# The last input load moved from SyncE's DMA queue to ScalarE's, behind two waits

## The chip, the cores and the metric

The kernel runs on one core of a Trainium2 chip. The metric is device time in microseconds (us), the median of several executions. The profile shows one execution, taken by the hardware profiler; its span is somewhat shorter than the time of that execution, and the table below gives both.

Engines are named as in the profile: PE is TensorE (matmuls), PEld its weight loads, DVE is VectorE, ACT is ScalarE, POOL is GpSimd, SP is SyncE. SP computes nothing here; it issues DMAs. The 16 DMA engines of the core move the data, whichever engine issued them.

## The reference

```
q, k : (8 batches, 8 heads, 512 rows, 64) float32
out[b, h] = q[b, h] @ k[b, h].T * (1 / sqrt(64))      # (8, 8, 512, 512) float32
```

The inputs are 8.4 MB each, the output is 67.1 MB.

## The kernel before

**Units and groups.** The work is cut into four *units* of two batches (`UNITS = 4`). A unit has one load of k (x = 0) and one of q (x = 1), each 2 MB as 128 partitions of 16 KB. They are called k0, q0 to k3, q3 here. Every unit gives four *groups* of output (`ALL = 16` groups, g = 0 to 15). A group is one store of 4 MB: 128 partitions, two rows of 16 KB each. The stores are called store 0 to store 15.

**Buffers.** There are three big buffers in SBUF of 4 MB each (`bigs`). A buffer holds either the raw q and k of a unit, or the finished output of a group:

```
    def xf(v):
        return bigs[(0, 1, 2, 1)[v]].rearrange("p x i k -> p (x i k)").rearrange(
...
    def store_buffer(g):
        return bigs[(0, 2, 1)[g % 3]]
```

So units 0, 1, 2 are loaded into buffers 0, 1, 2, and unit 3 goes into buffer 1 once unit 1 has been read out of it. Group 0 writes its output into buffer 0, group 1 into buffer 2 (where unit 2 was), group 2 into buffer 1 (where unit 3 was), group 3 into buffer 0 again, and so on.

**Stages.** POOL casts what has been loaded to bf16 (line 122, two casts for each load, `ready` is raised by one when both are done). PE transposes the cast data through PSUM (`turn`, line 130), eight transposes at a time. ACT and DVE copy the transposed words into `kT` and `qz` (`move`, line 184), each for its half of the partitions. PE then makes the scores of a group as eight pairs of matmuls of 128x512 (`scores`, line 145). Even pairs are taken out of PSUM, scaled, by ACT (line 209), odd pairs by DVE (line 212), into the buffer of the group. Each raises its semaphore, `act` or `dve`, by one for every pair.

**Order.** Each engine has an order written out by hand; an engine waits in it until a semaphore has reached a constant.

- SP: six loads k0 to q2 at once; then it waits for `ready >= 3` (both casts of k1 done) and issues k3 over k1; then for `ready >= 4` (casts of q1 done) and issues q3 over q1; then for each group it waits until ACT and DVE have raised their semaphores by four each, and issues the store (lines 95 and 96). At the end it waits for the stores.
- POOL: the casts in the order k0, q0, ..., k3, q3, each behind the landing of its load.
- PE: in each group the first three pairs, then the transposes of the chunk four groups ahead (`c = g + CHUNKS`), then the other five pairs. Before the second matmul of a group it makes sure that the group's buffer is free:

```
                if g < 3:
                    pe.wait_ge(sem["ready"], (2, 6, 8)[g])
                else:
                    pe.wait_ge(store_sems[g % 3], g // 3 * 16)
```

  Group 1 thus waits for the casts of q2 (`ready >= 6`), group 2 for those of q3 (`ready >= 8`), the later ones for the store that used the buffer last (group 3 for store 0, group 4 for store 1).
- ACT and DVE: `evacuator`, with `parity` 0 for ACT and 1 for DVE. It first moves the first four chunks; then, group by group, it evicts its four pairs of the eight, with the moves of one chunk in between.

Of the kernel before, what the change touches and what calls it, by code (L numbers as in the profile page):

```python
# [5 lines left out]
def kernel(  # L6
# [5 lines left out]
    nc = tc.nc  # L12
# [3 lines left out]
    UNITS = B // 2  # L16
# [21 lines left out]
    sem = {name: nc.alloc_semaphore(name) for name in names}  # L38
    load_sems = [nc.alloc_semaphore(f"load{n}") for n in range(2 * UNITS)]
# [3 lines left out]
    q_r = q.rearrange("(v b) g (m j) d -> v (b g m) (j d)", b=2, j=R)  # L43
    k_r = k.rearrange("(v b) g (m j) d -> v (b g m) (j d)", b=2, j=R)
# [25 lines left out]
    def xf(v):  # L70
        return bigs[(0, 1, 2, 1)[v]].rearrange("p x i k -> p (x i k)").rearrange(
            "p (x s c) -> p x s c", x=2, s=2)

    def store_buffer(g):
        return bigs[(0, 2, 1)[g % 3]]

    def load(v, x):
        return nc.sync.dma_start(out=xf(v)[:, x],
                                 in_=(k_r, q_r)[x][v].rearrange("p (s c) -> p s c", s=2)
                                 ).then_inc(load_sems[2 * v + x], 16)  # L80


    tc.no_tile_sem_insts.add(load(0, 0).ins.name)
    tc.close()
    tc.compile()  # L85


    for n in range(1, 2 * (UNITS - 1)):
        load(n // 2, n % 2)
    for x in range(2):  # L90
        nc.sync.wait_ge(sem["ready"], 3 + x)
        load(UNITS - 1, x)
    for g in range(ALL):
        nc.sync.wait_ge(sem["act"], 4 * g + 4)
        nc.sync.wait_ge(sem["dve"], 4 * g + 4)  # L95
# [59 lines left out]
    for g in range(ALL):  # L155
        c = g + CHUNKS
# [12 lines left out]
    def move(copy, c, s, tile_):  # L169
        v, t = divmod(c, CHUNKS)  # L170
        n0 = v % 2 * N
        h0 = t % 2 * W
        if t < 2:
            src = tile_[half(s)].rearrange("d j (n h m) -> d h n m j", n=N, h=2)
        else:
            src = tile_[half(s)].rearrange("d (i jj) (n h m) -> d h i n m jj", jj=JJ, n=N, h=2)
            h0 = t % 2 * IW
        for h in range(2):
            if t < 2:
                dst = kw[half(h), n0:n0 + N, :, s, h0:h0 + W]  # L180
            else:
                dst = qw[half(h), n0:n0 + N, h0:h0 + IW, h * U // 2:(h + 1) * U // 2].rearrange(
                    "d n i (m s jj) -> d s i n m jj", s=2, jj=JJ)[:, s]
            copy(out=dst, in_=src[:, h]).then_inc(sem["moved"], 1)  # L184

    def evacuator(engine, copy, scaled, parity, done, freed):
        if parity:
            for v in range(2):
                engine.memset(qz[:, v * N:(v + 1) * N], 0.0).then_inc(sem["zeroed"], 1)  # L189
        for c in range(CHUNKS):  # L190
            engine.wait_ge(sem["turn"], c + 1)
            if c == 2:
                engine.wait_ge(sem["zeroed"], 2)
            move(copy, c, parity, first[c])
        count = 0
        for g in range(ALL):
            o = store_buffer(g)
            for p in range(parity, PAIRS, 2):
                x, i = p // 4, p % 4 * 2
                count += 1  # L200
                engine.wait_ge(done, count)
                scaled(o[:, x, i:i + 2, :], pss[(PAIRS * g + p) % 3]).then_inc(freed, 1)
                c = g + CHUNKS
                if p in (1, 2) and c < ALL:
                    engine.wait_ge(sem["turn"], c + 1)
                    move(copy, c, parity, tp)

    evacuator(nc.scalar, nc.scalar.copy,
              lambda o, ps: nc.scalar.mul(out=o, in_=ps, mul=scale),  # L209
              0, sem["pe_act"], sem["act"])  # L210
    evacuator(nc.vector, nc.vector.tensor_copy,
              lambda o, ps: nc.vector.tensor_scalar(out=o, in0=ps, scalar1=scale, scalar2=None,  # L212
                                                    op0=mult),
# [31 lines left out]
```

## Time and profile before

| What | Value |
|---|---|
| Time, median of 3 runs | 201.15 us (201.14 to 201.38) |
| The profiled execution's own time | 201.16 us |
| Its span | 199.8 us |
| Granted TensorE clock, mean | 0.827 of full speed |
| Busy: PE, DVE, ACT, POOL | 98.2, 106.1, 84.7, 39.5 us |
| Moved by DMA | 83.95 MB, mean 420 GB/s |
| Read from HBM, written to HBM | 16.78 MB, 67.11 MB |
| Issue to landing, median: store, k load, q load | 21.8, 15.4, 17.8 us |

How to read it: the page gives the busy time of each engine, then a strip in 40 slices of 5 us (a digit is the busy share of a slice in tenths, and a row gives the rate of the DMA engines in GB/s), then the queues, the chain of work that ended last, and groups of instructions by line. Every line of the chain and of a timeline begins with its start in us and its length in us. "Issue to landing" is the time from the start of the issuing instruction until the last part of the data has been reported as landed; with several transfers queued it holds the waiting in the queue too. `q1` is the queue on which SP's DMAs run.

### The profile page before, as it was taken

To read this page: it belongs to the slowest core of one execution; us is meant where nothing else is said; L and a number is where in the kernel's file an instruction comes from. 1 tells how busy PE (TensorE), PEld (TensorE's weight loads), DVE (VectorE), ACT (ScalarE), POOL (GpSimd) and SP (SyncE) were. 2 spreads that over 40 slices of the span, in tenths; PEclk is the share of its full clock that TensorE was granted. 3 is DMA by queue.
4 is the path that set the end of the run, shared out by engine and by line. 5 is a ranking of instruction groups with operands and counts; after the bars stand their busy time and mean duration, and the time that the engine had idled before them with its cause. 6 is when DMAs were issued, how large, how long until landed. Compare 5 with 4: busy or idle time off the path is not lost.

```text
span 199.8 us, 1074 instructions
## 1 busy us (share of the span) xinstructions
PE 98.2 (49%) x377; PEld 46.7 (23%) x384; DVE 106.1 (53%) x98; ACT 84.7 (42%) x97; POOL 39.5 (20%) x22
## 2 busy tenths in 40 slices
PE   0027660375695637676547646873737373720000
PEld 0026530141442314243124313330202020200000
DVE  4815691074798928476917682767364545440000
ACT  2004670264686726465626653664444343520000
POOL 1299999986000000000000000000000000000000
PEclk9999996578799978889957995799696969685555
DMA  6999999999999999999999999999999999999996
GB/s 207 433 436 426 430 433 433 430 387 430 426 443 426 426 425 431 439 430 423 426 443 433 426 423 436 436 430 423 430 443 430 423 426 436 433 426 430 436 426 275
DMA packets 5509, 83.95 MB, mean 420 GB/s; under 512 B 384, under 2 KB 384, under 8 KB 384
## 3 DMA queue, kind: packets, MB, share of 16 engines
q1 hardware_dynamic: 5504, 83.89, 98.7%
q8 instruction: 3, 0.05, 0.1%
q14 instruction: 2, 0.02, 0.0%
HBM read 16.78 MB, written 67.11 MB: 420 GB/s over the span
## 4 chain that ended last, share of the span: by engine, by line
DMA 53%; DVE 12%; POOL 12%; PE 9%; issue 1%; ACT 1%; SPq 0%
DMA out_dram<-big 42%; POOL xb L122 12%; DVE big L212 10%; DMA big<-in_q_dram 8%; PE ps L145 7%; DMA big<-in_k_dram 4%; PE tp L130 3%; DVE qz L184 2%; DVE kT L184 1%; ACT big L209 1%; SPq L95 0%
## 5 line engine op out<-in xcount | busy, mean ns | idle before, releaser
L145 PE MATMUL ps<-kT,qz 128*128 128x512 bf16 x249 | 78.4, 447 | 63.0 <-DMA out_dram<-big 31.1
L212 DVE TENSOR_SCALAR big<-ps 128x1024 f32<-128x1024 f32 x64 | 77.0, 1223 | 52.0 <-PE ps L145 49.9
L209 ACT ACTIVATE big<-ps 128x1024 f32<-128x1024 f32 x64 | 64.9, 1024 | 71.1 <-PE ps L145 67.9
L145 PEld LDWEIGHTS ps<-kT,qz 128*128 128x128 bf16 x256 | 24.8, 108 | 109.7 <-DMA out_dram<-big 34.5
L122 POOL CAST xb<-big 128x2048 bf16<-128x2048 f32 x16 | 38.8, 2466 | 7.0 <-DMA big<-in_k_dram 6.0
L130 PE MATMUL tp<-identity,xb 128*128 128x128 f32 x104 | 18.9, 343 | 13.6 <-POOL xb L122 13.6
L130 PEld LDWEIGHTS tp<-identity,xb 128*128 128x128 f32 x104 | 17.2, 184 | 17.6 <-issue 16.5
L184 DVE COPY kT<-tp 64x512 f32<-64x512 f32 x14 | 9.7, 694 | 9.0 <-PE tp L130 8.5
L184 ACT COPY kT<-tp 64x512 f32<-64x512 f32 x14 | 8.1, 577 | 14.1 <-PE tp L130 14.0
L184 DVE COPY qz<-tp 64x512 f32<-64x512 f32 x12 | 8.3, 694 | 4.4 <-PE tp L130 4.1
L189 DVE MEMSET qz<- 128x4096 uint32 x2 | 6.9, 3472 | 3.6 <-PEq L85 2.8
L184 ACT COPY qz<-tp 64x512 f32<-64x512 f32 x12 | 7.5, 622 | 2.0 <-PE tp L130 1.8
L130 PE MATMUL ps<-identity,xb 128*128 128x128 f32 x24 | 5.4, 412 | 1.2 <-POOL xb L122 1.2
L130 PEld LDWEIGHTS ps<-identity,xb 128*128 128x128 f32 x24 | 5.0, 226 | 1.6 <-POOL xb L122 1.6
L184 DVE COPY qz<-ps 64x512 f32<-64x512 f32 x4 | 2.8, 695 | 1.9 <-PE ps L130 1.7
L184 ACT COPY qz<-ps 64x512 f32<-64x512 f32 x4 | 2.5, 626 | 2.2 <-PE ps L130 2.2
L184 ACT ACT_TABLE_LOAD x1 | 1.3, 1283 | 1.9 <-PEq L85 1.9
L184 DVE COPY kT<-ps 64x512 f32<-64x512 f32 x2 | 1.4, 694 | 0.3 <-PE ps L130 0.3
L184 ACT COPY kT<-ps 64x512 f32<-64x512 f32 x2 | 1.2, 578 | 0.5 <-PE ps L130 0.5
L102 POOL MEMSET identity<- 128x128 f32 x1 | 0.2, 205 | 1.5 <-POOLq L85 1.5
L104 POOL TENSOR_SCALAR_AFFINE_SELECT identity<-identity 128x128 f32<-128x128 f32 x1 | 0.3, 294 | 0.2 <-POOL identity L102 0.2
L229 POOL MEMSET const-float32-0.0<- 128x1 f32 x1 | 0.1, 100 | 0.2 <-issue 0.2
(3 smaller groups left out, 0.3 us busy)
## 6 DMA issues: line engine op xcount, KB each, us to landing
out_dram<-big SPq DMA_DIRECT2D x16, 4096.0 KB, 21.8
big<-in_k_dram SPq DMA_DIRECT2D x4, 2048.0 KB, 15.4
big<-in_q_dram SPq DMA_DIRECT2D x4, 2048.0 KB, 17.8
```

Of the source, the lines that this page charges most:

```text
L102: nc.gpsimd.memset(identity, 0.0).then_inc(sem["ident"], 1)
L104: nc.gpsimd.affine_select(out=identity, in_=identity, compare_op=mybir.AluOpType.not_equal, fill=1.0, base=0, pattern=[[-1, P]], channel_m ...
L122: cast = nc.gpsimd.tensor_copy(out=dst, in_=src)
L130: ins = pe.transpose(out=dst[:, w], identity=identity, in_=xw[:, c % SLOTS * W + w])
L145: ins = pe.matmul(out=pss[pair % 3][:, w, :], lhsT=qz[:, n, i + w], rhs=keys[:, n], start=True, stop=True)
L184: copy(out=dst, in_=src[:, h]).then_inc(sem["moved"], 1)
L189: engine.memset(qz[:, v * N:(v + 1) * N], 0.0).then_inc(sem["zeroed"], 1)
L209: lambda o, ps: nc.scalar.mul(out=o, in_=ps, mul=scale),
L212: lambda o, ps: nc.vector.tensor_scalar(out=o, in0=ps, scalar1=scale, scalar2=None, op0=mult),
L229: nc = _bacc.Bacc("TRN2", target_bir_lowering=False, num_devices=1)
```

## The change

`load` gets the issuing engine as an argument. SP's order loses the wait for `ready >= 4` and the load of q3: it goes from k3 straight to the stores. ACT's order gets three things between its last eviction of group 0 and its first of group 1: the wait for `ready >= 4`, a wait for the landing of k3 (`load_sems[6] >= 16`), and the issue of q3 on ACT's own DMA queue. The data, the buffers and all other waits are as before.

```
-    def load(v, x):
-        return nc.sync.dma_start(out=xf(v)[:, x],
-                                 in_=(k_r, q_r)[x][v].rearrange("p (s c) -> p s c", s=2)
-                                 ).then_inc(load_sems[2 * v + x], 16)
+    def load(v, x, queue=nc.sync):
+        return queue.dma_start(out=xf(v)[:, x],
+                               in_=(k_r, q_r)[x][v].rearrange("p (s c) -> p s c", s=2)
+                               ).then_inc(load_sems[2 * v + x], 16)
...
-    for x in range(2):
-        nc.sync.wait_ge(sem["ready"], 3 + x)
-        load(UNITS - 1, x)
+    nc.sync.wait_ge(sem["ready"], 3)
+    load(UNITS - 1, 0)
     for g in range(ALL):
         nc.sync.wait_ge(sem["act"], 4 * g + 4)
         nc.sync.wait_ge(sem["dve"], 4 * g + 4)
...
             for p in range(parity, PAIRS, 2):
                 x, i = p // 4, p % 4 * 2
+                if g == 1 and p == 0:
+                    engine.wait_ge(sem["ready"], 4)
+                    engine.wait_ge(load_sems[2 * UNITS - 2], 16)
+                    load(UNITS - 1, 1, engine)
                 count += 1
                 engine.wait_ge(done, count)
                 scaled(o[:, x, i:i + 2, :], pss[(PAIRS * g + p) % 3]).then_inc(freed, 1)
```

## The prediction

> **What bounds the kernel now.** I first read the head of the page: the busy strip of the DMA engines, the rate and the queue.
>
> ```profile
> span 199.8 us, 1074 instructions
> ...
> DMA  6999999999999999999999999999999999999996
> GB/s 207 433 436 426 430 433 433 430 387 430 426 443 426 426 425 431 439 430 423 426 443 433 426 423 436 436 430 423 430 443 430 423 426 436 433 426 430 436 426 275
> ...
> q1 hardware_dynamic: 5504, 83.89, 98.7%
> ```
>
> The 16 DMA engines are busy in every slice but the first and the last, at about 430 GB/s, and one queue (SP's) carries everything. 83.89 MB at 430 GB/s is 195 us of the 199.8. So the transfers are the bound: the kernel is lengthened only by an idle stretch of the DMA engines or by a slower rate, and shortened only by removing such a stretch or a dip. There is one dip in the middle (387, slice 9), which the windows view places:
>
> ```profile
> 36.00:40.00 4.00, 2.01 (x5) 0.81 (x6) 0.52 (x1) 1.02 (x1) 3.92 (x2) 0.50 1.03 438
> 40.00:42.00 2.00, 2.00 (x10) 1.79 (x9) 0.71 (x1) 1.02 (x1) 2.00 (x2) 0.50 0.96 319
> 42.00:52.00 10.00, 6.30 (x26) 3.19 (x24) 6.19 (x6) 5.26 (x6) 5.72 (x3) 0.84 1.00 429
> ```
>
> The last column is GB/s. 319 instead of 430 for 2 us is 0.5 us lost, as the last load gives way to the first store.
>
> Next, who needs the moved load (q3: input q, fourth unit). The chain of waits has it, and the timelines of SP and ACT have the issues around it:
>
> ```profile
> 28.23 15.33 DMA big<-in_q_dram
> 43.57 0.05 issue
> 43.62 4.85 POOL xb L122 x2
> 48.47 0.05 issue
> 48.52 1.96 PE ps L145 x5
> ...
> 57.28 0.03 issue
> ```
>
> ```profile
> 23.32 0.33 SPq L78 DMA_DIRECT2D big<-in_k_dram  x1
> 28.23 0.33 SPq L78 DMA_DIRECT2D big<-in_q_dram  x1
> ```
>
> ```profile
> 30.95 0.40 SPq L96 DMA_DIRECT2D out_dram<-big  x1
> ```
>
> ```profile
> 57.32 0.37 SPq L96 DMA_DIRECT2D out_dram<-big  x1
> ```
>
> ```profile
> 29.20 1.03 ACT L209 ACTIVATE big<-ps 128x1024 f32<-128x1024 f32 x1 [1.06 <-PE ps L145]
> 38.63 1.02 ACT L209 ACTIVATE big<-ps 128x1024 f32<-128x1024 f32 x1 [8.40 <-PE ps L145]
> ```
>
> Columns: start, length, what. q3 lands at 43.57; POOL casts it until 48.47; only then may TensorE go past the first matmul of group 2 (ready >= 8, since group 2's results overwrite the buffer that q3 was cast from); 57.32 issues store 2. The chain up to there is serial. It is harmless now because transfers are queued ahead: by the DMA view split by time, k3 lands 14.6 us after 23.32 (37.9), store 0 22.3 us after 30.95 (53.3), store 1 16.4 us after 47.15 (63.6), store 2 16.0 us after 57.32 (73.3), store 3 19.0 us after 63.93. Store 1's data ends about 61.9 (below), so store 2, issued 57.32, comes 4.6 us early. **That slack is what the change spends.**
>
> **What the Trainium skill says.** (1) "DMA: Bandwidth & Descriptors", section "Issuing engines are not separate DMA queues": DMAs of all issuing engines run on the same 16 DMA engines and interleave; a second issuer saves only issue time. The trace before has one queue, so it shows neither; its rate leaves no idle engine to fill. (2) Same page, "Where 436 GB/s comes from": a ceiling of 435 GB/s. The trace agrees: 423 to 443 by slice. (3) Same page, "Queues, rings and completion order": each DMA engine takes turns between the queues that have work, a packet at a time, a packet being typically 9-17 descriptors. No run here shows how long a turn is. A load is 128 rows of 16 KB, 8 per engine, a store 16 per engine, so a turn may be one 16 KB descriptor or a whole transfer's share. This is my main unknown. (4) Same page, "Latency and other measured facts": about 0.6 us to the first byte. The trace differs: the first load is issued at 0.74, and the DMA view cut by time has no packet before 1.75 and one in 1.75:1.80, so I use 1.0 us.
>
> **The change, part by part.**
>
> *SP loses a wait and an issue.* SP no longer waits for ready >= 4 (28.22) and issues q3 (0.33 us). SP's next work, store 0, waits for the evictions of group 0 and goes at 30.95 in either case: worth 0. But store 0 now stands directly behind k3 in SP's queue, and the 16 engines, leaving k3 at about 37.0 (it lands 37.9), go straight to its 9.8 us of data (4.19 MB at 429). No gap arises there, since it was issued 6 us earlier.
>
> *ACT gains two waits and an issue.* ACT is done with group 0 at 29.20 + 1.03 = 30.23; ready >= 4 holds since 28.22, k3's landing comes at 37.95. ACT then issues at about 38.0, for 0.33 to 0.40 us (SP's rows), until 38.4. Behind it in ACT's order is its first eviction of group 1, which starts at 38.63 anyhow, since TensorE itself waits for ready >= 6 until 37.98. Cost 0; at worst, if ACT's issue takes 1 us, 0.8 us late for group 1. Those who wait for that eviction are TensorE (it frees PSUM) and SP (store 1). Store 1 goes at 47.15 and is needed when store 0 and q3 end, after 51, so 4 us cover it.
>
> *q3 shares the engines with store 0.* Issue 38.0 + 1.0 = 39.0 first packets. With turns of one 16 KB descriptor q3 gets half of 430 GB/s: 2.10 MB at 215 GB/s = 9.8 us, so 48.8, and about 1.0 for the spread over engines and the completion (k3: data end near 37.0, landing 37.95): **q3 lands at about 49.8 instead of 43.57, 6.2 us later.** Bounds: it can't beat the whole rate, 39.0 + 4.9 + 1.0 = 44.9; if store 0's share is drained first it starts at 46.8 and lands at 46.8 + 4.9 + 1.0 = 52.7; if mixed reads and writes ran all the time at the dip's 319 GB/s, 39.0 + 4.19 MB/319 + 1.0 = 53.1. I take 49.8, since a packet in the page's count (5504 for 83.89 MB) is one 16 KB row.
>
> *The serial chain moves by the same amount.* Casts 49.85 to 54.7 (2 x 2.42), group 2 from 54.75, then 57.32 - 48.47 = 8.85 us of its own to the issue: 63.6. Its data start at 63.6 + 1.0 = 64.6.
>
> *What the engines have meanwhile.* From 37.0: store 0, q3 and store 1, 10.49 MB at 429 = 24.4 us, to 61.4; before, with the dip's 0.5, to 61.9. So the engines are idle from about 61.4 to 64.6, **some 3 us**. The break-even is q3 landing at 64.6 - 61.9 = 2.7 us before 49.8, 47.1: any later and each us costs a us.
>
> *Nothing gives it back, nothing adds to it.* After store 2 groups follow at about 6.6 us (57.32 to 63.93), transfers at 9.8. Group 3 needs store 0's landing (53), is ready at 70.2, store 2's data last to 74.4; group 4 needs store 1 (63) and is ready by 77, needed at 84. The order before returns, late by the gap. The bubble cannot be made up, for the engines have no other slack.
>
> Sum: transfers after store 1 start at 64.6 instead of 61.9, +2.7 us. The profiled execution took 201.16 us, 1.3 around its span of 199.8; the median is 201.15, so nothing to shift. 201.16 + 2.7 = **203.9 us**. The uncertainty of landing (49.3 to 50.6) gives 203.4 to 204.7.
>
> **The rivals.**
>
> *Turns of a whole share.* q3 waits for store 0 on every engine and lands at 52.7; group 2 and store 2 move 2.9 us further: 206.8. For it speaks the skill's 9-17 descriptors, the count of a load or store per engine with its completion; against it that rows are counted singly.
>
> *Mixed traffic is slow.* The dip's rate throughout the shared stretch: landing 53.1, so 207.2. For it speaks the 319 GB/s; against it that one changeover was over in 2 us.
>
> *The new queue is served ahead (the other side).* If q3 gets well over half of each engine, it lands at 44.9 to 47.1, store 2 is in the queue before store 1's data end, there is no bubble, and the dip's 0.5 us may go as the load no longer ends against the store: 200.6 to 201.2. It decides from a landing before 47.1. Against: nothing prefers a queue.
>
> *The change doesn't do what it says.* If ACT got through its waits later than 38.0, q3 would slip one for one; its instructions ahead end at 30.23, so I see no reason. Nor can the transfers be beside each other for nothing: no rate is free.
>
> **How the numbers follow.** Fair turns 0.66 (203.9), whole share 0.16 (206.8), slow mixing 0.08 (207.2), served ahead 0.10, half of that within 0.2% and half faster. 0.2%, 0.4 us, is about what a measurement of this kernel can tell from no change. The range 202.2 to 207.1 goes from fair turns with q3 landing at 48.1 to the slow cases; it leaves out the served-ahead case and a half of slow mixing, about 15 in 100. Slower 0.90, same 0.05, faster 0.05.
>
> **What would show it.** Right: a second queue with 2.10 MB; q3 some 12 us from issue to landing on ACT, landing near 50; POOL idle from 43 until then and its last two casts ending near 55; group 1's evictions in place; store 2 issued near 63.6, landing some 12 us later instead of 16.0; the only slice of low GB/s between 61 and 65; the stretch after store 2 as long as before. A landing near 53 says whole shares or slow mixing, and the rate between 39 and 50 tells them apart. Wrong: no gap near 62, or group 2 starting before 50, or gaps that recur with later stores.

## The result and the profile after

The changed kernel takes 208.69 us (median of 6), the kernel before 201.28 us on the same chip: ratio 1.0381, 95% interval 1.0349 to 1.0413. That is slower, as forecast, but by 7.4 us where 2.7 were forecast, and outside the range. The profiled execution took 209.6 us with a span of 208.3.

The head of its page: the busy strip of the DMA engines, the rate, and the queues (packets, MB, share of the 16 engines).

```profile
span 208.3 us, 1082 instructions
...
DMA  6999999999980899999999999999999999999996
GB/s 217 425 441 422 441 422 422 406 431 428 434 346 3 352 450 404 442 412 431 422 409 447 412 441 412 444 412 441 415 444 406 441 415 441 415 434 422 431 431 261
...
q1 hardware_dynamic: 5360, 81.79, 92.9%
q10 hardware_dynamic: 144, 2.10, 2.4%
```

The second queue carries its 2.10 MB, and there is the hole: slice 12 moves 3 GB/s. The windows view cuts it finer (columns: stretch; its length; busy time and count of PE, PEld, DVE, ACT, POOL; clock; DMA share; GB/s).

```profile
52.00:61.00 9.00, 2.34 (x7) 1.04 (x8) 0.84 (x1) 1.02 (x1) 4.81 (x2) 0.50 1.01 433
61.00:62.00 1.00, 1.00 (x6) 1.00 (x5) 0.38 (x1) 0.99 (x1) 0.00 (x0) 0.50 0.41 164
62.00:68.00 6.00, 4.60 (x19) 1.67 (x18) 5.16 (x6) 4.04 (x6) 0.00 (x0) 0.91 0.01 5
68.00:72.00 4.00, 2.58 (x16) 1.50 (x14) 3.65 (x5) 3.49 (x5) 0.00 (x0) 1.00 0.93 393
```

Store 1's data end between 61 and 62, as worked out; nothing moves until 68. The forecast hole was 3 us, this one is over 6. The chain of waits says what it waited for, and SP's timeline gives the issue of store 2:

```profile
39.77 13.97 DMA big<-in_q_dram
53.74 0.05 issue
53.79 4.83 POOL xb L121 x2
58.61 0.05 issue
58.66 2.31 PE ps L144 x5
...
67.78 0.03 issue
```

```profile
67.82 0.37 SPq L95 DMA_DIRECT2D out_dram<-big  x1
```

Landing of q3, two casts, group 2, store 2: the chain is the forecast one, but q3 lands at 53.74 and not at 49.8. ACT's side is as forecast too: its issue takes 0.37 us, and the eviction behind it follows at once.

```profile
39.77 0.37 ACTq L78 DMA_DIRECT2D big<-in_q_dram  x1
40.19 1.94 ACT L214 ACTIVATE big<-ps 128x1024 f32<-128x1024 f32 x2 [9.40 <-DMA big<-in_k_dram]
```

In this execution k3 landed late (39.7). The change does not force that: in a second profile of the same kernel, told below, k3 landed at 38.1, q3 at 52.4, and the span was 206.9. I use that one for the sums. Its own time, 208.29 us, is 0.4 us under the median.

### The profile page after: what moved, and what is told of

Its sections match the earlier page's. It is cut to its first block, busy times and chain, and to the rows that moved or that the text cites. A ratio compares the mean times of both kernels' runs of the same rounds, so it can differ in the third digit from the quotient of the medians.

```text
span 208.3 us, 1082 instructions
## 1 busy us (share of the span) xinstructions
PE 98.7 (47%) x384; PEld 46.2 (22%) x384; DVE 106.1 (51%) x98; ACT 84.6 (41%) x97; POOL 39.5 (19%) x22
## 4 chain that ended last, share of the span: by engine, by line
DMA 59%; DVE 11%; PE 11%; POOL 7%; issue 1%; SPq 0%; ACTq 0%
DMA out_dram<-big 39%; DMA big<-in_q_dram 13%; DVE big L217 9%; PE ps L144 8%; DMA big<-in_k_dram 8%; POOL xb L121 7%; PE tp L129 3%; DVE qz L183 2%; DVE kT L183 1%; SPq L94 0%; ACTq L203 0%
## 5 line engine op out<-in xcount | busy, mean ns | idle before, releaser
L144 PE MATMUL ps<-kT,qz 128*128 128x512 bf16 x256 | 79.1, 444 | 70.7 <-DMA out_dram<-big 29.3
```

The costliest lines, as they stand in the source:

```text
L144: ins = pe.matmul(out=pss[pair % 3][:, w, :], lhsT=qz[:, n, i + w], rhs=keys[:, n], start=True, stop=True)
```

## The experiments

Two theories stood at first. Theory 1: only q3's landing counts, each us beyond the break-even is an idle us of the DMA engines. Theory 2: a second queue, or loads mixed with stores, costs by itself.

### The second queue or the place in line

**No wait for k3's landing.**

```
                 if g == 1 and p == 0:
                     engine.wait_ge(sem["ready"], 4)
-                    engine.wait_ge(load_sems[2 * UNITS - 2], 16)
                     load(UNITS - 1, 1, engine)
```

> The changed kernel without ACT's wait for the landing of k3; ACT still issues q3 on its own queue. Theory 1 (what counts is when q3 lands; every us beyond the break-even of about 47 us is an idle us of the DMA engines after store 1): ACT issues at 30.3, so q3 shares the engines with k3 and the first part of store 0 and lands at 42 to 46, store 2 is queued in time, 201.0 to 201.6 us. Theory 2 (a second queue beside the stores costs by itself, through mixed reads and writes or a slower rate after it): still 203 us or more.

Measured 203.29 us, ratio 1.0105 (1.0088 to 1.0123). That is not theory 1's number; it lies where theory 2 put it (203 us or more), but it does not need theory 2's cause. ACT issued at 29.83 and q3 landed at 45.3, as expected; but the chain has another load in front:

```profile
23.49 19.69 DMA big<-in_k_dram
43.18 0.05 issue
43.23 9.58 POOL xb L121 x4
52.82 0.05 issue
52.86 2.31 PE ps L144 x5
```

Sharing with q3 put k3 at 43.2 instead of 38, and POOL then had four casts to do, 9.58 us. Group 2 was let go at 52.8, 4.4 us later than before, and store 2 went at 62.03, just too late: store 1's data end between 61 and 62. My expectation had followed q3 and forgotten k3. Whether the second queue has a cost of its own as well, this run alone does not settle; the run with both edits below does.

**q3 on SP's queue, behind store 0.**

```
     for g in range(ALL):
+        if g == 1:
+            nc.sync.wait_ge(sem["ready"], 4)
+            load(UNITS - 1, 1)
         nc.sync.wait_ge(sem["act"], 4 * g + 4)
```

(and nothing issued by ACT)

> q3 issued by SP on SP's queue, directly behind store 0, with no wait for k3's landing; ACT issues nothing. Theory 1: strictly in order q3 lands at about 37.5 + 9.8 + 4.9 + 1 = 53 to 54, as late as the changed kernel has it on its own queue (53.7), so about 207.5 to 208.7 us: the second queue and the sharing are not the cause, being behind store 0 is. Theory 2 (the second queue costs by itself): clearly under 207 us.

Measured 209.01 us, ratio 1.0386 (1.0368 to 1.0403), the changed kernel's 1.0381. q3 landed at 53.4, store 2 went at 67.52. Strictly behind store 0 on one queue costs what the second queue beside it costs: the sharing brought q3's landing 1.0 us forward at best (52.4 in the second profile), and nothing that the times can tell.

**Half of group 2 freed from q3.**

```
+            if g == 2 and p == 4 and w == 1:
+                pe.wait_ge(sem["ready"], 8)
             if p == 0 and w == 1:
                 if g < 3:
-                    pe.wait_ge(sem["ready"], (2, 6, 8)[g])
+                    pe.wait_ge(sem["ready"], (2, 6, 7)[g])
```

> The changed kernel with group 2's wait split: its first four pairs, which overwrite the half of the buffer that held k3, wait for the casts of k3 only (ready >= 7), the last four for those of q3 (ready >= 8). q3 lands as late as before, about 53.7, but only half of group 2 hangs on it. Theory 1: store 2 goes 4 to 5 us earlier (about 63.3 instead of 67.8), so 203.7 to 204.7 us. Theory 2 (second queue or mixing slows the engines themselves): 207 us or more.

Measured 205.11 us, ratio 1.0198 (1.0183 to 1.0213). q3 landed at 53.85, as late as ever, and SP's timeline has store 2 4.6 us earlier than in the changed kernel's first profile, 3.2 us earlier than in its second (the line merges stores 2 and 3; its start is store 2's issue):

```profile
63.26 7.01 SPq L95 DMA_DIRECT2D out_dram<-big  x2
```

So it is the chain from q3 to store 2, and not the late load as such. The time came 0.4 us above the expected band.

**Both: no wait for k3's landing, and the split.** Both edits above together. The theory 4 of the expectation, that only an idle stretch of the engines costs anything, comes up again under "The other 2.6 us".

> ACT issues q3 on its own queue without waiting for k3's landing, and group 2's wait is split (first four pairs behind the casts of k3, last four behind those of q3). In the run without the landing wait the casts of k3 ended near 48 and those of q3 at 52.8; with the split store 2 should go at about 57.5 and be queued before store 1's data end at 61 to 62. Theory 1 with theory 4 (only an idle stretch of the engines costs; a second queue and mixed loads and stores cost nothing): no idle stretch, 200.8 to 201.5 us, as the kernel before. Theory 2 (a second queue or the mixing costs by itself): 202 us or more.

Measured 201.22 us, ratio 1.0005 (0.9997 to 1.0013). The rate on its page has no hole:

```profile
GB/s 207 426 429 433 436 429 423 429 397 446 429 426 423 426 446 426 426 426 443 426 426 429 436 436 429 423 426 446 426 429 423 433 443 423 423 429 443 423 429 269
```

q3 still runs on ACT's queue, mostly beside k3; only its last packets run beside store 0. So a second queue costs nothing by itself. What a load mixed with a store costs this run hardly tests; the changed kernel's second profile does, further down, where q3 and store 0 run side by side at 431 GB/s in 43:50. With both, theory 2 falls: the hole is the cost. Nor is there a gain; this version equals the kernel before.

### Why q3 landed so late

**Store 0 held until k3 has landed.**

```
+    nc.sync.wait_ge(load_sems[2 * UNITS - 2], 16)
     for g in range(ALL):
         nc.sync.wait_ge(sem["act"], 4 * g + 4)
```

> The changed kernel with SP holding store 0 until k3 has landed, so that store 0 and q3 are issued at the same time on two empty queues. In the changed kernel q3's first packets came 3.8 us after its issue. Theory 3 (store 0's descriptors already taken up by the engines stand ahead of it): q3 starts about 1 us after its issue, shares evenly and lands at about 51, store 2 goes 2 to 3 us earlier, about 206 us, after a gap of 1 to 1.5 us near 39. Rival (a first transfer on ACT's queue is slow to start whatever stands there): q3 again starts 3.8 us after its issue and lands at 53 or later, 208 us or more.

Measured 206.40 us, ratio 1.0258 (1.0243 to 1.0274), as theory 3 has it. ACT issued q3 at 38.22, it landed at 50.8. The DMA view for 38:40 of this run:

```profile
q1 hardware_dynamic: 16, 0.26, 44.7%
q10 hardware_dynamic: 4, 0.07, 13.8%
```

Here the engines take one packet of store 0 each, and q3's (q10) first packets follow 1.8 us after the issue, not after the 1 us that theory 3 had. The packets of store 0, on an empty queue, begin 0.9 us after their issue (38.16 to 39.08).

**The changed kernel again**, with no edit.

> The changed kernel once more, for a second profile beside these two: k3 landed 1.2 to 1.5 us later in its first profile (39.7) than in other runs with the same order of loads (38.2 to 38.3). If that was chance, k3 lands near 38.3, q3 near 53, store 2 some 0.5 to 1 us earlier, and the profiled execution takes 208.3 to 208.8 us; the stretch from store 2's landing stays at 129.2 us. If the change itself delays k3, it lands near 39.7 again.

Measured 208.72 us, ratio 1.0374 (1.035 to 1.0398). The chain and SP's timeline of its profile have q3's issue and landing, its casts, and the issue of store 2; the windows view has the hole:

```profile
38.19 14.19 DMA big<-in_q_dram
52.38 0.05 issue
52.43 4.82 POOL xb L121 x2
```

```profile
66.47 0.37 SPq L95 DMA_DIRECT2D out_dram<-big  x1
```

```profile
62.00:67.00 5.00, 3.86 (x15) 1.28 (x15) 4.87 (x6) 3.69 (x4) 0.00 (x0) 0.93 0.00 0
```

The DMA view for 38.2:41.8, then 41.8:42.2, then 43:50 (packets, MB, share):

```profile
q1 hardware_dynamic: 96, 1.57, 101.8%
...
q10 hardware_dynamic: 7, 0.11, 66.8%
q1 hardware_dynamic: 5, 0.08, 47.7%
...
DMA packets 184, 3.01 MB, mean 431 GB/s; under 512 B 0, under 2 KB 0, under 8 KB 0
...
q10 hardware_dynamic: 95, 1.56, 51.8%
q1 hardware_dynamic: 89, 1.46, 48.6%
```

For more than 3.6 us after the issue not one packet of q3 starts (the first comes after 3.7 us, at 41.9); 96 packets of store 0 do, six for each of 16 engines. After that the two queues share evenly. Put end to start, the packets of each engine in the trace go one of store 0, one of q3, one of store 0, and so on, until q3's eight are through. So the turns are single 16 KB packets, as I had assumed, but it takes six of the other queue's packets until q3's come in, 2.7 us more than the 1.0 us that I had used. That an engine has taken those up ahead is my reading of it. The run with store 0 held shows that most of the delay goes when nothing stands there. It is not special to stores: where q3 was issued beside k3, in the two runs without the wait for its landing, its first packets came 3.5 us after the issue. The run with store 0 held also gives the price of lateness: from it to this one q3's landing moves 50.8 to 52.4, and store 2's issue 64.86 to 66.47, 1.6 us each.

### The other 2.6 us

From store 2's landing (issue plus time to landing) to the end of the span, the kernel before takes 199.8 - 73.3 = 126.5 us, the changed one 208.3 - 79.1 = 129.2, and so it is, within 0.2 us, in all runs with a hole so far. The same 13 stores, and no second hole. The clearest case is the run without the wait for k3's landing: its store 2 landed at 73.3, as in the kernel before, and the span was 2.7 us longer all the same.

**The wait for k3 alone, on SP's queue.**

```
     load(UNITS - 1, 0)
+    nc.sync.wait_ge(sem["ready"], 4)
+    nc.sync.wait_ge(load_sems[2 * UNITS - 2], 16)
+    load(UNITS - 1, 1)
```

> Only the wait for k3's landing, on SP's own queue: SP issues k3, waits for its landing, issues q3, then the stores; ACT issues nothing. q3 runs alone and lands near 45, so there can be no idle stretch after store 1; the engines stand still once, for about 1.5 us near 38, before q3. Theory 4 (after the engines have all stood still and started together, the stores to the end run 2.6 us longer, 129.2 us instead of 126.5 from store 2's landing to the end of the span, whatever caused the stop): 1.5 + 2.6, so about 205 us and a bare second of it in the gap itself. Rival (the 2.6 us belong to the second queue or to q3's lateness): about 202.7 us.

Measured 204.51 us, ratio 1.0164 (1.015 to 1.0178), between the two, and for another reason than either gave. The stretch from store 2's landing is 126.8 us, so a stop ahead of a load did not bring the 2.6; but the stop cost 3.3 us and not 1.5:

```profile
36.00:38.00 2.00, 0.17 (x1) 0.13 (x2) 0.00 (x0) 0.00 (x0) 1.93 (x2) 0.50 0.33 139
38.00:40.00 2.00, 2.00 (x6) 0.74 (x5) 0.67 (x1) 1.02 (x1) 2.00 (x1) 0.50 0.73 156
```

The queue stands empty from the last data of k3 (near 37) until its landing is reported (37.8) and q3's first packets come, near 39, and those are slow: the engines are 0.73 busy for 156 GB/s, where running loads take 1.03 for 438 (36:40 in the kernel before). Theory 4, that any stop does it, falls.

**A stop ahead of store 2, in the kernel before.**

```
         nc.sync.wait_ge(sem["dve"], 4 * g + 4)
+        if g == 2:
+            nc.sync.wait_ge(store_sems[1], 16)
```

> The kernel before, with one wait added: SP issues store 2 only when store 1 has landed (63.6). No second queue, q3 as early as before; the engines stand still once, before a store. The stop itself: store 2 lands about 11.3 us after its issue (as in the changed kernel), near 75.0 instead of 73.3, +1.7. Theory 5 (stores that start on all engines together after a stop run longer to the end, 129.2 us from store 2's landing instead of 126.5): +1.7 + 2.6, so 205.2 to 205.8 us. Rival (the longer stretch needs the second queue or q3's lateness): 202.5 to 203.1 us.

Measured 205.18 us, ratio 1.0191 (1.0176 to 1.0206), at the edge of what theory 5 gave and far from the rival. The sum came out, but not by its terms: the stop moved store 2's landing by 2.6 us (75.9) and not by 1.7, and the stretch after it took 128.0 us and not 129.2. What carries theory 5 is that the stretch grew at all. q3 landed at 43.2, as early as ever, and no second queue exists. The windows view of this run and, under it, 110 us of the later stores:

```profile
60.00:62.00 2.00, 0.92 (x4) 0.31 (x4) 2.00 (x2) 0.96 (x2) 0.00 (x0) 1.00 0.65 279
62.00:64.00 2.00, 1.11 (x5) 0.40 (x5) 1.38 (x2) 0.94 (x2) 0.00 (x0) 1.00 0.02 8
64.00:66.00 2.00, 2.00 (x15) 1.40 (x14) 1.68 (x2) 2.00 (x3) 0.00 (x0) 1.00 0.96 393
...
80.00:190.00 110.00, 61.27 (x214) 25.16 (x216) 61.45 (x57) 50.84 (x56) 0.00 (x0) 0.79 1.01 426
```

The same 110 us in the kernel before, and in the changed kernel's second profile:

```profile
80.00:190.00 110.00, 58.05 (x208) 23.80 (x209) 58.41 (x54) 48.53 (x53) 0.00 (x0) 0.81 1.01 430
```

```profile
80.00:190.00 110.00, 62.25 (x224) 25.64 (x226) 62.35 (x58) 51.83 (x58) 0.00 (x0) 0.81 1.01 426
```

One stop ahead of a store, and the stores after it run at 426 GB/s instead of 430 to the end; 1% of 127 us is some 1.25 us. The records of landings say the same: from the first engine's landing of store 2 to the first engine's landing of the last store it takes 126.5 us in the kernel before and 127.7 to 127.8 with the stop alone and in the changed kernel. The rest of the 2.6 is a matter of spread. In the same records, store 2 reaches its last engine 1.7 us after its first in the kernel before, but 0.2 us after it behind the hole of the changed kernel; at the last store it is 1.7 and 1.6 us again. A hole lets the stragglers catch up, and the spread then grows back, which counts as 1.4 us if one starts from the last landing. With the stop alone the spread was still 1.4 us at store 2, so its stretch holds little but the slower stores. In the run without the wait for k3 the last landing, 73.3, hides the whole hole: the first engine landed 1.6 us later than in the kernel before (73.1 against 71.6). Side by side (landings are read to 0.1 us, as issue plus time to landing):

| Run | Store 2 issued | landed | from there to the end | GB/s in 80:190 |
|---|---|---|---|---|
| Before | 57.32 | 73.3 | 126.5 | 430 |
| No wait and split (no hole) | 56.56 | 73.2 | 126.7 | 430 |
| No wait for k3 (bare stop ahead of store 2) | 62.03 | 73.3 | 129.2 | 427 |
| Wait alone (stop ahead of a load) | 60.35 | 76.5 | 126.8 | 430 |
| Stop ahead of store 2 | 63.41 | 75.9 | 128.0 | 426 |
| Changed, second profile | 66.47 | 77.8 | 129.1 | 426 |

With the wait alone store 2 lands 3.2 us later than in the kernel before, and the stores after it are not slower; so lateness by itself is not what slows them.

**The hole filled with useless traffic.** In the changed kernel; the spare tensor lies in HBM.

```
         nc.sync.dma_start(out=out_r[g], ...).then_inc(store_sems[g % 3], 16)
+        if g == 1:
+            nc.sync.wait_ge(sem["ready"], 6)
+            for n in range(2):
+                nc.sync.dma_start(out=spare[n], in_=xw[:, 8 * W:11 * W].rearrange("p w c -> p (w c)")
+                                  ).then_inc(spare_sems[n], 16)
```

> The changed kernel with useless traffic in its idle stretch: behind store 1 SP also writes 3.1 MB of cast input to a spare tensor in HBM (two transfers of 12 KB rows, 7.3 us at 430 GB/s), which nothing reads. Store 2 cannot start earlier for it. Theory 4 (the 2.6 us after store 2 come from all 16 engines standing still and starting together): the engines run on in their own steps, the stretch from store 2's landing to the end goes back to about 126.5 us, and the kernel gets about 2 us faster than the changed one (206.5 us) although it moves 3.1 MB more. Rival (the later stores are slower for another reason): as slow as the changed one or slower, 208.7 to 209.7 us.

Measured 208.64 us, ratio 1.0367 (1.0351 to 1.0383): not the 206.5 expected, and not to be told from the changed kernel. The useless writes landed only at 70.9 on the last engine, later than the hole would have ended, so store 2 landed at 80.5; from there it took 127.2 us instead of 129.2. The windows view (80:125, then 125:190) has the rate of the kernel before at first, and later less, with no second stop:

```profile
80.00:125.00 45.00, 27.93 (x113) 13.74 (x115) 28.66 (x29) 24.67 (x29) 0.00 (x0) 0.85 1.01 430
125.00:190.00 65.00, 36.70 (x114) 12.98 (x116) 34.24 (x31) 27.86 (x29) 0.00 (x0) 0.78 1.01 428
```

So the total says nothing, because the useless writes were too long for the hole. The shorter stretch comes in the main from the spread, which at store 2 was 1.8 us here and 0.2 behind the hole. From the first engine's landing to the first engine's landing it is 127.2 us, between the 126.5 of the kernel before and the 127.8 of the changed one. Engines kept running thus lose less afterwards, but the rate can fall to 428 GB/s without a stop as well, for a reason that these runs do not show.

**Half of the engines held up.** Theory 6: engines that start in step hinder each other. A small useless transfer of 8 rows stands right ahead of store 2, first in the changed kernel, then in the kernel with the stop alone:

```
+        if g == 2:
+            nc.sync.dma_start(out=spare, in_=xw[0:8, 5 * W:10 * W].rearrange("p w c -> p (w c)")
+                              ).then_inc(spare_sem, 16)
...
+            nc.sync.dma_start(out=spare, in_=xw[0:P:16, 6 * W:10 * W].rearrange("p w c -> p (w c)")
+                              ).then_inc(spare_sem, 16)
```

> The changed kernel with one small useless transfer of 8 rows of 20 KB right ahead of store 2 on SP's queue, into a spare tensor that nothing reads: it should hold up half of the engines by some half of a packet's 0.61 us, so that the engines start store 2 in two steps and not in one; it also makes store 2 0.4 us later. Theory 6 (the engines' common step makes the later stores slow: a packet takes 618 ns on average after the stop, 612 in the kernel before): most packets at 611 ns again and a store every 9.72 us instead of 9.83, at least 1 us less from store 2's landing to the end. Rival (the step doesn't matter): 618 ns and 129.2 us as in the changed kernel.

Measured 210.85 us, ratio 1.047 (1.0439 to 1.0501). The 8 rows of 20 KB, from 8 neighbouring partitions, took 2.9 to 3.6 us each instead of some 0.75, so eight engines were held up by some 3 us, and the half step that was wanted did not come about. The rate of the later stores was 427 GB/s all the same.

> The kernel before with the stop ahead of store 2 (SP waits for store 1's landing), and right ahead of store 2 a useless transfer of 8 rows of 16 KB, now from partitions 16 apart, into a spare tensor. It should take half of the engines about 0.6 to 0.9 us and leave them 0.3 to 0.5 us behind the other half, in another part of the 0.61 us of a packet. Theory 6 (engines that start in step make the later stores slow): packets back to 612 to 614 ns on average instead of 618, the stretch of the engine that ends first from store 2 to the last store back from 127.7 to about 126.6 us, in all 204.3 to 205 us. Rival (the step doesn't matter): 618 ns, 127.7 us, 205.5 to 206 us.

Measured 206.44 us, ratio 1.0265 (1.0248 to 1.0282). Not theory 6's 204.3 to 205, and above the rival's 206 too, since the useless transfer held store 2 up. From partitions 16 apart the rows of 16 KB took 1.1 to 2.0 us; the two transfers differ in row length as well, so what made them slow is not told apart. The engines' first packets after the stop, useless rows included, started over 0.7 us (64.78 to 65.47), more than a packet's 0.61 us, where with the stop alone they started within 0.15; but a packet still took 617 ns on average (618 with the stop alone, 612 in the kernel before):

```profile
80.00:190.00 110.00, 64.45 (x225) 26.38 (x223) 61.40 (x58) 51.49 (x57) 0.00 (x0) 0.76 1.01 427
```

So scattered starts don't help; nothing here speaks for theory 6. That a stop ahead of a store is followed by slower stores is shown; why is open.

## Why the prediction was wrong

**Right in kind.** Transfers bound the kernel; SP's lost wait and ACT's three additions cost nothing (0.37 us of issue, the eviction behind it at once); the landing of q3, the casts, group 2 and store 2 form the serial chain; the engines run dry between 61 and 62; each us beyond that is an idle one; there is one hole only. The even shares by 16 KB packet were right as well, though named the main unknown.

**Wrong in size.** By the second profile, whose span is 206.9:

- *"Issue 38.0 + 1.0 = 39.0 first packets"* is the term that failed in the sum for q3. First packets came at 41.9, 3.7 us after the issue at 38.2, when six packets of store 0 had gone ahead on each engine. The 1.0 us was taken from the first load, which met an empty queue; q3 met busy engines. q3 landed at 52.4 and not at 49.8: 2.6 us.
- *Group 2* took 66.47 - 52.38 = 14.1 us from landing to issue, 13.8 forecast: right. The start of store 2's data, 1.0 us forecast, took 0.9 (the first packet in the trace at 67.4): right too. From the end of the issuing instruction, at 66.84, it is 0.5 us, and only counted so is the first byte near the 0.6 us that the Trainium skill gives ("DMA: Bandwidth & Descriptors", section "Latency and other measured facts"). The first load, from which I took the 1.0, is no different: its issue began at 0.74 and took 0.39 us, and its first packet came at 1.76.
- *"Nothing adds to it"* failed. From store 2's landing on I had taken the time of before; it was 129.1 us instead of 126.5, 2.6 more. Of that 1.25 us are slower stores. The rest is the spread that the hole had taken out, which is a part of the hole's own cost that the last landing hides.

The sum closes: store 2 landed 4.5 us later (77.8 against 73.3), and 2.6 us were added after it, 7.1; the spans differ by 206.9 - 199.8 = 7.1. In the prediction's own terms, by the start of store 2's data, the hole was 67.4 - 61.9 = 5.5 us where 64.6 - 61.9 = 2.7 were forecast. What the forecast lacked, 7.1 - 2.7 = 4.4 us, is 2.6 us of landing, 0.2 of group 2 and the start together, 1.25 of slower stores, and some 0.3 that I cannot place.

One sum of the prediction is off without effect: an issue of 1 us on ACT, from 38.0, would have made group 1 0.4 us late (39.0 against 38.63), and not 0.8.

**The rivals.** A turn of a whole share gave the same landing (52.7) by another mechanism; the packets that alternate one by one rule it out, and so it shows that a landing alone would not have told the two apart. Slow mixing falls with the 431 GB/s of 43:50, where q3 and store 0 ran side by side. A queue served ahead was seen nowhere. The gain that I gave the vanishing dip (0.5 us) did not come: the dip moved to the end of k3, 352 GB/s in 36:38 of the first profile.

## What to carry to other kernels

A transfer on another queue does not come in at once: where other transfers keep the engines busy it starts some packets late, then gets half of the rate, so put a load that a serial chain waits for ahead of bulk stores, not beside them. Before moving it, work out the break-even from the chain behind it to the moment when the engines run dry, and count every load that shares with it (k3 here), not the moved one alone. Price a stop of the DMA engines at more than its length: with the stop alone no packet ran from 62.9 to 64.3, 1.4 us, and the kernel lost 4.0 us.

## What the runs showed of the hardware that was not expected

- Where the other queue kept the engines busy, the first packet of a second queue came 3.5 to 3.7 us after the issue; on empty engines it came after 1.8 us, with one store packet ahead. From then on each engine took one 16 KB packet of either queue in turn.
- After a stop ahead of a store the stores ran at 426 GB/s instead of 430 (426 or 427) until the end, in every run that had such a stop; the stop ahead of a load, in the one run that had it alone, left 430.
- After a stop ahead of a load, that load's first data were slow (0.73 busy for 156 GB/s), and the stop cost 3.3 us.
- 8 rows of 20 KB from 8 neighbouring partitions took 2.9 to 3.6 us, 8 rows of 16 KB from partitions 16 apart 1.1 to 2.0 us, where a 16 KB packet of a full store takes 0.61. Why is not shown.
